# A down product by Strassen's identity in the last half of a two-layer decoder step

## The chip, the cores and the metric

The kernel runs on one core of one Trainium2 chip. The metric is the device time of one execution in microseconds (us), the median of several runs. TensorE is called PE in the profile, VectorE DVE, ScalarE ACT, GpSimd POOL and SyncE SP.

## The reference

One inference step of a hybrid decoder: 1024 prompt tokens and 8 sample tokens (1032 in all, `D_MODEL` 1024) go through a layer of convolution mixers and a layer of attention mixers, all in float32. Each is followed by an MLP with squared ReLU and `D_FF` = 4096:

```
def sqrelu_mlp(h, w1, w2):
    return jnp.square(jax.nn.relu(h @ w1)) @ w2
...
hp = hp + rmsnorm(sqrelu_mlp(rmsnorm(hp, g[2]), mlp_w1[layer], mlp_w2[layer]), g[3])
```

The change concerns the last of these MLPs, for the second half of the tokens, which ends the program.

## The kernel before

Features lie on partitions, tokens in the free dimension. The tokens are cut into three blocks, 512, 256 and 264 wide (`BW`). Half 0 is block 0, half 1 blocks 1 and 2. `Net.mlp` does one layer's MLP for one half and is called four times; the last call (half 1 of layer 1) is the last work of the program, save for the norm, the residual and the store.

Float32 matmuls are done in three: every operand is split into a high part of type fp32r (a cast on ACT) and a low part (what is left, a `tensor_sub` on DVE), and high by high, high by low and low by high are accumulated in one PSUM bank (`project`, and the same three lines in `down`). There are 41 buffers of 128 x 1056 (`unit`), 10 of 128 x 528 (`small`) and 8 PSUM banks.

`mlp` goes over the 4096 hidden features in eight chunks of 512, that is four tiles of 128. In a chunk `up` makes the four hidden tiles for the blocks of the half: 24 matmuls for each tile and block, then relu, square and the high part on ACT, the low part on DVE. Then `down` multiplies them with the chunk's four tiles of w2: eight output tiles `ct` for each block, 12 matmuls each. DVE adds each result from its bank to the accumulator `acc` in SBUF. The weights come by DMA in tiles of 128 x 1024 (`Weights`), are loaded up to three ahead and split up to two ahead. In the last chunk block 1 is finished first, up and down, and then block 2.

Every engine works through its instructions in the order in which they were emitted, and waits at the first whose operands aren't there. That order is set by `Pace`: an estimate of each engine's clock, from costs per element in `cost`. The main strand emits the matmuls; all else (splits, copies out of banks) are tasks, each of which goes on when the estimated clock of TensorE has passed the time that the task asked for. So where an instruction stands in its engine's queue is settled when the program is built. All of the kernel's instructions bear line 75, where `Engine` passes them on (line 77 in the changed kernel), and are told apart by the names of their tiles.

Of the kernel before, what the change touches and what calls it, by code (L numbers as in the profile page):

```python
# [10 lines left out]
F32 = mybir.dt.float32  # L11
# [6 lines left out]
P = 128  # L18
# [24 lines left out]
PE_NS, HOPS = 1.02 / 2400, 0.15  # L43

# [20 lines left out]
class Engine:  # L65
    """Passes calls on to an engine and keeps the estimate of its clock."""
# [20 lines left out]
class Pace:  # L87
    """Order of emission. Every engine issues its instructions in the order in which they are emitted, so
    independent strands of work are kept as tasks (generators), and a task goes on when the estimated clock
    of the tensor engine has reached the time that it asked for. The main strand is plain code."""  # L90
# [13 lines left out]
    def cost(engine, what, kw, aps):  # L104
# [14 lines left out]
        return 0.1 + n * 3.4 / 1000  # L119
# [44 lines left out]
    def soon(self):  # L164
        """when what was emitted last is ready"""
        return self.last + self.HOP
# [28 lines left out]
class Room:  # L195
    """Tiles of one size, given out and taken back by hand: the one that has been still for longest is next."""
# [17 lines left out]
class Feat:  # L214
    """Features of a block of tokens: units of KP feature tiles."""
# [9 lines left out]
class Weights:  # L225
    """The weights' tiles in the order of their use: loaded ahead, and split into high and low parts."""
# [7 lines left out]
    def advance(self):  # L234
        net, items = self.net, self.items
        while (self.loaded < len(items) and self.loaded - self.taken < self.limit
               and net.has_unit(self.back, 1 + 2 * self.whole)):
            src, n = items[self.loaded]
            x = net.take("raw", F32, self.back)
# [5 lines left out]
    def split(self, i, x, n):  # L245
# [9 lines left out]
        self.ready[i] = (h, l)  # L255

# [22 lines left out]

class Squares:  # L280
    """Sum of the squares of a block's feature tiles, by partition, as the tiles come."""
# [4 lines left out]
    def add(self, x, gain=None):  # L286
        """x: emitted last; scaled by the gain afterwards, where given"""
# [19 lines left out]
class Net:  # L307
# [29 lines left out]
    def weight_order(self):  # L337
# [7 lines left out]
        for i in range(2):  # L345
            for hf in range(2):
                for ch in range(NF // 4):
                    main.extend((io["w1"][i, 4 * ch + f], 1024) for f in range(4))
                    main.extend((io["w2"][i, 4 * ch + f], 1024) for f in range(4))
# [19 lines left out]
    def unit(self, name, dt=F32):  # L369
        """for the main strand"""  # L370
# [3 lines left out]
    def unit_later(self, name, dt=F32, back=True):  # L374
        """for tasks"""
# [39 lines left out]
    def bank_later(self, name="mm", spare=SPARE):  # L415
        """for tasks"""
# [4 lines left out]
    def table(self, name):  # L421
        """the set of the scalar engine's functions that follow"""
# [1455 lines left out]
```

## Time and profile before

| | us |
|---|---|
| three runs | 2210.55, 2209.44, 2217.82 (median 2210.55) |
| span of the profiled execution (no other time of it is given) | 2208.2 |
| TensorE busy | 2162.6 (98%) |
| DVE, ACT, POOL busy | 1481.2 (67%), 1084.4 (49%), 148.0 (7%) |
| TensorE's granted clock, mean of the span | 0.995 |

Busy time is a mean over stages. In the last half, which begins at 1824.9 us, the matmuls follow each other without a gap to 2195.1; then the last norm, residual and store. A matmul's own duration (0.28 us) is longer than its spacing, since they are pipelined; its price is the spacing.

### The profile page before, as it was taken

Reading aid. Unit: us, or ns where it says so; the run is one execution under the profiler, and the core shown is the slowest. Engines: PE = TensorE matmul, PEld = TensorE weight load, DVE = VectorE, ACT = ScalarE, POOL = GpSimd, SP = SyncE. Lnnn points to the kernel's source line nnn. Section 1 sums busy time; section 2 is a strip of 40 time slices with the busy share of each in tenths; the row PEclk is TensorE's granted clock in tenths of the full one; section 3 lists DMA queues with packets and bytes.
Section 4 is the critical chain, followed back from the end, with each engine's and each line's share of the span. In section 5 each row is a group of like instructions: output and inputs, shape, how many; then the busy total and the mean of one; then the engine's idle time right before and its main releaser. Section 6 shows DMA issues by size and latency. Waiting matters only on the chain. (4 is left out here: it accounts for less than half of the span.)

```text
span 2208.2 us, 35620 instructions
## 1 busy us (share of the span) xinstructions
PE 2162.6 (98%) x14039; PEld 1963.4 (89%) x14039; DVE 1481.2 (67%) x2762; ACT 1084.4 (49%) x2206; POOL 148.0 (7%) x253
## 2 busy tenths in 40 slices
PE   5999999999999999999999999999999999999997
PEld 4987898889888988999989989988887989999997
DVE  8885588984754756787658675667876585444446
ACT  6124354345543633788544463366874554334234
POOL 2131010010000011000000002201000000000000
PEclk9999999999999999999999999999999999999999
DMA  4113544352533444323343443532342455222231
GB/s 179 49 58 97 170 172 154 96 182 87 175 103 124 142 140 153 106 86 126 118 139 133 131 139 119 187 123 84 122 124 98 130 163 169 90 87 87 87 101 64
DMA packets 85255, 269.97 MB, mean 122 GB/s; under 512 B 16904, under 2 KB 19096, under 8 KB 84904
## 3 DMA queue, kind: packets, MB, share of 16 engines
q1 hardware_dynamic: 74528, 223.16, 31.5%
q0 software_dynamic: 10560, 44.54, 5.3%
q8 instruction: 110, 1.80, 0.3%
q14 instruction: 57, 0.47, 0.1%
HBM read 234.87 MB, written 44.83 MB: 127 GB/s over the span
## 5 line engine op out<-in xcount | busy, mean ns | idle before, releaser
L75 PE MATMUL mm<-xh,w 128*128 128x256 f32 (+2 forms) x4720 | 1086.8, 320 | 2.7 <-DVE xl L75 2.7
L75 PEld LDWEIGHTS mm<-xh,w 128*128 128x128 f32 x4720 | 788.6, 189 | 68.5 <-issue 2.9
L75 PE MATMUL mm<-hid,w 128*128 128x512 f32 (+2 forms) x4608 | 751.6, 321 | 0.0
L75 PE MATMUL mm<-xl,w 128*128 128x256 f32 (+2 forms) x2360 | 751.1, 318 | 0.0
L75 PEld LDWEIGHTS mm<-hid,w 128*128 128x128 f32 x4608 | 658.7, 188 | 65.5 <-issue 2.7
L75 DVE TENSOR_TENSOR w<-raw,w 128x1024 fp32r<-128x1024 f32 (+1 forms) x330 | 395.1, 1207 | 166.6 <-ACT w L75 166.4
L75 PEld LDWEIGHTS mm<-xl,w 128*128 128x128 f32 x2360 | 446.8, 189 | 31.5 <-issue 1.2
L75 ACT CAST w<-raw 128x1024 fp32r<-128x1024 f32 (+1 forms) x350 | 355.0, 1033 | 66.5 <-PE mm L75 44.5
L75 ACT ACTIVATE relu<-mm 128x256 f32<-128x256 f32 (+2 forms) x192 | 87.8, 457 | 408.6 <-PE mm L75 403.3
L75 DVE TENSOR_TENSOR acc<-acc,mm 128x256 f32<-128x256 f32 (+2 forms) x336 | 166.5, 508 | 133.8 <-PE mm L75 132.1
L75 DVE TENSOR_TENSOR hid<-mm,hid 128x256 fp32r<-128x256 f32 (+2 forms) x192 | 98.7, 514 | 219.8 <-ACT hid L75 219.0
L75 ACT ACTIVATE mm<-relu 128x256 f32<-128x256 f32 (+2 forms) x192 | 88.7, 462 | 6.1
L75 ACT ACTIVATE hid<-relu 128x256 fp32r<-128x256 f32 (+2 forms) x192 | 91.2, 475 | 0.0
L75 DVE SCALAR_TENSOR_TENSOR cv<-ga,small,cv 128x512 f32<-128x512 f32 x120 | 83.3, 744 | 0.0
L75 DVE SCALAR_TENSOR_TENSOR taps<-ga,small,taps 128x482 f32<-128x482 f32 (+29 forms) x120 | 78.6, 731 | 0.0
L75 ACT COPY qk<-mm 128x512 f32<-128x512 f32 (+2 forms) x39 | 17.4, 446 | 106.2 <-PE mm L75 101.3
L75 ACT COPY y<-mm 128x512 f32<-128x512 f32 (+2 forms) x48 | 21.4, 446 | 91.7 <-PE mm L75 91.7
L75 PE MATMUL mm<-mixh,w 128*128 128x512 f32 (+2 forms) x288 | 64.9, 320 | 0.0
L75 DVE TENSOR_TENSOR sq<-sq 128x264 f32<-128x264 f32 (+2 forms) x84 | 43.0, 512 | 29.9 <-ACT sq L75 29.0
L75 ACT CAST ph<-pt 128x512 fp32r<-128x512 f32 (+1 forms) x80 | 41.1, 522 | 34.8 <-PE pt L75 32.3
L75 ACT CAST xh<-norm 128x256 fp32r<-128x256 f32 (+2 forms) x104 | 41.4, 425 | 33.6 <-DVE norm L75 33.1
L75 POOL TENSOR_TENSOR w<-raw,w 128x1024 fp32r<-128x1024 f32 x20 | 50.5, 2543 | 108.3 <-ACT w L75 106.7
(235 smaller groups left out, 2091.6 us busy)
## 6 DMA issues: line engine op xcount, KB each, us to landing
raw<-w SPq DMA_DIRECT2D x256, 512.0 KB, 3.8
raw<-wic SPq DMA_DIRECT2D x32, 512.0 KB, 4.5
raw<-wia SPq DMA_DIRECT2D x26, 512.0 KB, 3.5
res<-res SPq DMA_DIRECT2D x18, 512.0 KB, 4.1
raw<-woc SPq DMA_DIRECT2D x16, 512.0 KB, 3.7
o_d_s<-c_d POOLq DMA_DIRECT2D x8, 1023.5 KB, 16.6
qscr<-qk POOLq DMA_DIRECT2D x26, 256.0 KB, 2.3
res<-y POOLq DMA_DIRECT2D x12, 512.0 KB, 3.9
```

What stands on the lines that cost most here:

```text
L75: r = fn(*args, **kw)
```

## The change

`FAST` says which chunks of which MLP half are done in the new way: of layer 1, half 1, chunks 0 to 6. In such a chunk the down product is taken as a product of 2 x 2 blocks, for each half `hc` of the output features: weights by two halves of the output columns and two halves of the chunk's hidden features (a11, a12, a21, a22), hidden tiles by two halves of the features and the two token blocks (r11, r12, r21, r22; block 1 is padded with zeros to 264). Strassen's identity in Winograd's form makes it with seven block products of sums instead of eight. `PRODUCTS` names them by the hidden side: 11, t1, 21, 22, t3, t2, t4.

`Weights.combine` loads two tiles of w2 for each `hc`, makes four sums on POOL, and splits the seven weight blocks (tiles `wp`): high part on ACT, low part on POOL and DVE in turn. `sums_chunk` leaves the squared hidden tiles in `hid`, makes four sums on DVE and splits the seven hidden blocks (tiles `t`). Each block product is 24 matmuls of 264 columns into two banks, and `collect` adds each bank to one of seven tiles `total` (in chunk 0 ACT copies it). After chunk 6 `join_totals` makes the accumulators from the totals with 14 sums on POOL. Chunk 7 is done as before. `Pace` counts a POOL operation at 2.5 ns an element in place of 3.4. Docstrings and comments went to blank lines, and `mlp` has the layer as a new argument; neither is shown.

```diff
+FAST = {(1, 1): (0, 7)}
+PRODUCTS = ("11", "t1", "21", "22", "t3", "t2", "t4")
...
-        return 0.1 + n * 3.4 / 1000
+        return 0.1 + n * 2.5 / 1000
...
+            if isinstance(src, tuple):
+                if not net.has_unit(self.back, 6 + 2 * self.whole):
+                    return
+                xs = [net.take("raw", F32, self.back) for _ in src]
+                for x, a in zip(xs, src):
+                    net.sp.dma_start(out=x[:, :n], in_=a)
+                self.whole += 2
+                self.ready[self.loaded] = parts = Parts(net)
+                net.pace.spawn(self.combine(self.loaded, xs, parts))
+                self.loaded += 1
+                continue
...
+    def combine(self, i, xs, parts):
...
+        net = self.net
+        yield net.pace.ready(*xs) + 0.1
+        while i - self.taken >= 4:
+            yield net.pace.now() + 0.3
+        block = lambda x, m: x[:, :1024].rearrange("p (f c) -> p f c", f=2)[:, :, m * 256:(m + 1) * 256]
+        a11, a21, a12, a22 = block(xs[0], 0), block(xs[0], 1), block(xs[1], 0), block(xs[1], 1)
+
+        def split(u, src):
+            h, l = parts.views(u)
+            net.act.copy(h, src)
+            yield net.pace.soon()
+            (net.dve if len(parts.units) % 2 else net.pool).tensor_sub(l, src, raw(h))
+            parts.units.append(u)
+
+        yield from split((yield from parts.unit()), a11)
+        small = yield from net.small("s1")
+        s1 = small[:, :512].rearrange("p (f c) -> p f c", f=2)
+        net.pool.tensor_add(s1, a21, a22)
+        net.pool.tensor_sub(a21, a11, a21)
+        at = net.pace.soon()
+        net.pool.tensor_sub(a11, s1, a11)
+        yield at
+        yield from split((yield from parts.unit()), s1)
+        net.drop(small)
+        u = yield from parts.unit()
+        yield from split(u, a12)
+        u = yield from parts.unit()
+        net.pool.tensor_sub(a12, a12, a11)
+        yield net.pace.soon()
+        yield from split(u, a12)
+        for src in (a21, a11, a22):
+            u = yield from parts.unit()
+            yield from split(u, src)
+        net.free(*xs)
+        self.whole -= 2
...
+class Parts:
...
+    DEPTH = 6
+
+    def __init__(self, net):
+        self.net, self.units, self.used, self.asked = net, [], 0, 0
+
+    def unit(self):
+        while self.asked - self.used >= self.DEPTH:
+            yield self.net.pace.now() + 0.2
+        self.asked += 1
+        return (yield from self.net.unit_later("wp", F32R, False))
+
+    @staticmethod
+    def views(u):
+        return [u[:, a * 512:(a + 1) * 512].rearrange("p (f c) -> p f c", f=2) for a in range(2)]
+
+    def get(self, n):
+        self.net.pace.wait(lambda: len(self.units) > n)
+        return self.views(self.units[n])
+
+    def done(self):
+        self.net.free(self.units[self.used])
+        self.used += 1
...
-                    main.extend((io["w2"][i, 4 * ch + f], 1024) for f in range(4))
+                    w2 = [io["w2"][i, 4 * ch + f] for f in range(4)]
+                    if self.fast(i, hf, ch):
+                        main.extend(((w2[hc], w2[hc + 1]), 1024) for hc in (0, 2))
+                    else:
+                        main.extend((w, 1024) for w in w2)
...
+    def mlp(self, layer, hf, xn, post, last=False):
         pace, W, bs = self.pace, self.W, HALVES[hf]
+        side_w = BW[bs[-1]] if hf else HT // 2
+        totals, outs = [], []
...
+        def sums_chunk(ch, first):
...
+            n = side_w
+            us, hi, lo, ready, raws, squared = {}, {}, {}, set(), {}, [0]
+            view = lambda u, o=0: u[:, o:o + 2 * n].rearrange("p (f t) -> p f t", f=2)
+
+            def raw_block(k):
+                s = yield from self.small("hid")
+                raws[k] = s
...
+            def hidden(f, b, ps):
+                yield pace.soon()
+                a = ps
+                self.act.activation(a, ps, AF.Relu)
+                yield pace.soon()
+                if hf:
+                    yield from squares(f, b - 1, a)
...
+            def split(k, src):
+                u = us[k] = yield from self.unit_later("t", F32R, False)
+                hi[k], lo[k] = view(u), view(u, 2 * n)
+                yield from self.split_later(hi[k], lo[k], src)
+                ready.add(k)
+
+            def left():
+                while squared[0] < 4:
+                    yield pace.now() + 0.2
+                yield pace.soon()
+                small = yield from self.small("t1")
+                t1 = view(small)
+                self.dve.tensor_sub(t1, view(raws["12"]), view(raws["11"]))
+                yield from split("11", view(raws["11"]))
+                yield from split("t1", t1)
+                self.drop(small)
+
+            def right():
+                while squared[0] < 8 or "11" not in ready:
+                    yield pace.now() + 0.2
+                yield pace.soon()
+                r11, r12, r21, r22 = (view(raws[k]) for k in ("11", "12", "21", "22"))
+                yield from split("21", r21)
+                self.dve.tensor_sub(r12, r22, r12)
+                yield from split("22", r22)
+                self.drop(raws["22"])
+                self.dve.tensor_add(r11, r12, r11)
+                self.dve.tensor_sub(r21, r21, r11)
+                yield pace.soon()
+                for k, t in (("t3", "12"), ("t2", "11"), ("t4", "21")):
+                    yield from split(k, view(raws[t]))
+                    self.drop(raws[t])
...
+            def collect(total, ps):
+                def emit():
+                    if first:
+                        self.act.copy(total, ps)
+                    else:
+                        self.dve.tensor_add(total, total, ps)
+                    self.banks.give(ps)
+
+                outs.append(pace.then(emit))
...
+            if first:
+                totals.extend(self.unit("total") for _ in PRODUCTS)
+            for hc in range(2):
+                parts = W.get()
+                for m, k in enumerate(PRODUCTS):
+                    h, l = parts.get(m)
+                    pace.wait(lambda: k in ready)
+                    bank = None
+                    for q in range(2):
...
+                            bank = self.bank()
...
+                        for f in range(2):
+                            wh, wl = (v[:, f, q * P:(q + 1) * P] for v in (h, l))
+                            self.pe.matmul(ps, lhsT=wh, rhs=hi[k][:, f], start=f == 0, stop=False)
+                            self.pe.matmul(ps, lhsT=wh, rhs=lo[k][:, f], start=False, stop=False)
+                            self.pe.matmul(ps, lhsT=wl, rhs=hi[k][:, f], start=False, stop=f == 1)
+                            pace.tick()
+                        if hf:
+                            collect(totals[m][:, (2 * hc + q) * n:(2 * hc + q + 1) * n], ps)
+                    if not hf:
...
+                    parts.done()
+                    if hc:
+                        self.free(us[k])
...
+        def join_totals(first):
...
+            pace.wait(lambda: all(t.done for t in outs))
+            if first:
+                for b in bs:
+                    acc[b] = self.feat(b, KD, "acc")
+            add, sub = self.pool.tensor_add, self.pool.tensor_sub
+            for hc in range(2):
+                m1, m5, m2, m3, m7, m6, m4 = (t[:, hc * 2 * n:(hc + 1) * 2 * n].rearrange("p (q t) -> p q t", q=2)
+                                              for t in totals)
...
+                def to(rows, side, x, y):
+                    if hf:
+                        v = acc[bs[side]].v[hc][:, 2 * rows:2 * rows + 2]
...
+                    c = slice(0, v.shape[-1])
+                    if first:
+                        add(v, x[:, :, c], y[:, :, c])
...
+                to(0, 0, m2, m1)
+                add(m6, m6, m1)
+                add(m5, m5, m6)
+                to(0, 1, m3, m5)
+                to(1, 1, m5, m7)
+                add(m7, m7, m6)
+                to(1, 0, m4, m7)
+            self.free(*totals)
...
+            if self.fast(layer, hf, ch):
+                at_start = ch == FAST[layer, hf][0]
+                sums_chunk(ch, at_start)
+                if not self.fast(layer, hf, ch + 1):
+                    join_totals(FAST[layer, hf][0] == 0)
+                continue
```

What it does to the order of instructions, at three places.

DVE before, in a middle chunk of the last half, from the low part of the last hidden tile (`hid`) to the first adds of the down product. `w` are low parts of weights, `acc` the adds from PSUM banks `mm`:

```order
L75 TENSOR_TENSOR hid_20351<-mm_20386,hid_20351 128x264
L75 TENSOR_TENSOR w_20428<-raw_20416,w_20427 128x1024
L75 TENSOR_TENSOR w_20431<-raw_20349,w_20430 128x1024
L75 TENSOR_TENSOR acc_18862<-acc_18862,mm_20420 128x256
L75 TENSOR_TENSOR acc_18864<-acc_18864,mm_20421 128x264
L75 TENSOR_TENSOR acc_18862<-acc_18862,mm_20422 128x256
```

DVE in the change, a middle chunk, from the first add after the up product. `mm_19998` and `mm_20009` are the two tiles of product 11, `mm_20021` and `mm_20030` those of t1; `t_20043` is hidden block 21:

```order
L77 TENSOR_TENSOR total_18863<-total_18863,mm_19998 128x264
L77 TENSOR_TENSOR total_18864<-total_18864,mm_20021 128x264
L77 TENSOR_TENSOR w_20004<-raw_19937,w_20003 128x1024
L77 TENSOR_TENSOR total_18863<-total_18863,mm_20009 128x264
L77 TENSOR_TENSOR total_18864<-total_18864,mm_20030 128x264
L77 TENSOR_TENSOR wp_20018<-raw_19855,wp_20018 128x512
L77 TENSOR_TENSOR t_20043<-hid_19921,t_20043 128x528
```

Before, the low part of the last hidden tile came ahead of all adds of the down product; now the low part of hidden block 21 comes behind four of them, a low part of w1 and one of block weights.

DVE in the change, right behind that. `t_20051` is block 22, `t_20091` t3, `hid` the sums, `mm_20053` and `mm_20066` product 21, `mm_20075` product 22:

```order
L77 TENSOR_TENSOR hid_19798<-hid_19990,hid_19798 128x528
L77 TENSOR_TENSOR t_20051<-hid_19990,t_20051 128x528
L77 TENSOR_TENSOR hid_19755<-hid_19798,hid_19755 128x528
L77 TENSOR_TENSOR hid_19921<-hid_19921,hid_19755 128x528
L77 TENSOR_TENSOR wp_20058<-raw_19854,wp_20058 128x512
L77 TENSOR_TENSOR total_18865<-total_18865,mm_20053 128x264
L77 TENSOR_TENSOR total_18865<-total_18865,mm_20066 128x264
L77 TENSOR_TENSOR total_18866<-total_18866,mm_20075 128x264
L77 TENSOR_TENSOR t_20091<-hid_19798,t_20091 128x528
```

All of it is new: three sums, three adds and a weights' low part stand between the low parts of 22 and of t3.

POOL in the change, the end of the same chunk's work (before, POOL has no such work in the last half). `wp_19909` and `wp_20025` are the fifth and the seventh weight block of the first `hc`, `wp_19996`, `wp_20047` and `wp_20177` the third, fifth and seventh of the second:

```order
L77 TENSOR_TENSOR wp_19909<-raw_19776,wp_19909 128x512
L77 MEMSET hid_19921 128x2x8
L77 TENSOR_TENSOR wp_19996<-raw_19855,wp_19996 128x512
L77 TENSOR_TENSOR raw_19855<-raw_19855,raw_19854 128x2x256
L77 TENSOR_TENSOR wp_20025<-raw_19777,wp_20025 128x512
L77 TENSOR_TENSOR wp_20047<-raw_19854,wp_20047 128x512
L77 TENSOR_TENSOR wp_20177<-raw_19855,wp_20177 128x512
```

Of the chunk's 16 operations, 13 stand before the low part of `wp_20025`, whose cast comes behind the end of the up product, as do those of the last two.

## Rows read from the trace of the kernel before

**Rows 1.** Head of the page: span, busy time and instructions of each engine.
```profile
span 2208.2 us, 35620 instructions
PE 2162.6 (98%) x14039; PEld 1963.4 (89%) x14039; DVE 1481.2 (67%) x2762; ACT 1084.4 (49%) x2206; POOL 148.0 (7%) x253
```
**Rows 2.** Windows, last half: length, busy PE, PEld, DVE, ACT, POOL, clock, DMA, GB/s.
```profile
1871.00:2148.00 277.00, 277.00 (x2307) 277.00 (x2307) 115.48 (x191) 100.39 (x194) 0.00 (x0) 1.00 0.27 92
```
**Rows 3.** Chain that ended last: start, length, what.
```profile
1831.31 343.01 PE mm L75 x2856
```
**Rows 4.** Timeline of PE, one chunk: start, duration, instruction.
```profile
1917.78 0.28 PE L75 MATMUL mm<-xh,w 128*128 128x256 f32 x1
...
1920.75 0.28 PE L75 MATMUL mm<-xl,w 128*128 128x264 f32 x1
...
1923.31 0.28 PE L75 MATMUL mm<-xl,w 128*128 128x264 f32 x1
...
1963.89 0.29 PE L75 MATMUL mm<-xh,w 128*128 128x256 f32 x1
```
**Rows 5.** Timeline of DVE: operations back to back, five sizes.
```profile
1752.19 1.28 DVE L75 TENSOR_TENSOR y<-y,res 128x512 f32<-128x512 f32 x2
...
1945.70 1.50 DVE L75 TENSOR_TENSOR acc<-acc,mm 128x256 f32<-128x256 f32 x4 [0.19 <-PE mm L75]
...
1952.92 2.35 DVE L75 TENSOR_TENSOR w<-raw,w 128x1024 fp32r<-128x1024 f32 x2
...
2199.64 0.71 DVE L75 TENSOR_TENSOR acc<-acc,rstd 128x528 f32<-128x528 f32 x1
2200.38 0.71 DVE L75 TENSOR_TENSOR acc<-acc,res 128x528 f32<-128x528 f32 x1
2201.01 0.70 DVE L75 TENSOR_TENSOR acc<-acc,rstd 128x528 f32<-128x528 f32 x1
```
**Rows 6.** Timeline of POOL, first stage: pairs of operations.
```profile
18.21 5.24 POOL L75 TENSOR_TENSOR w<-raw,w 128x1024 fp32r<-128x1024 f32 x2 [13.50 <-ACT w L75]
...
102.47 4.76 POOL L75 TENSOR_TENSOR w<-raw,w 128x1024 fp32r<-128x1024 f32 x2 [17.84 <-ACT w L75]
...
177.79 5.57 POOL L75 TENSOR_TENSOR w<-raw,w 128x1024 fp32r<-128x1024 f32 x2
```
**Rows 7.** Groups by form, ACT: count, busy us, mean ns, idle before.
```profile
L75 ACT ACTIVATE mm<-relu 128x264 f32<-128x264 f32 x32 | 12.7, 396 | 1.0
L75 ACT ACTIVATE relu<-mm 128x264 f32<-128x264 f32 x32 | 12.5, 391 | 54.9 <-PE mm L75 54.9
...
L75 ACT CAST mixh<-f 128x512 fp32r<-128x512 f32 x12 | 7.1, 590 | 13.6 <-DVE f L75 13.5
```
**Rows 8.** Timeline of DVE beside the pairs of rows 6.
```profile
19.02 2.25 DVE L75 SCALAR_TENSOR_TENSOR norm<-x,small,rstd 128x256 f32<-128x256 f32 x1
21.18 2.83 DVE L75 TENSOR_TENSOR total<-total,sq 128x512 f32<-128x512 f32 x1
...
104.05 0.43 DVE L75 TENSOR_TENSOR ga<-mm,ga 128x264 f32<-128x264 f32 x1
...
178.86 5.05 DVE L75 TENSOR_TENSOR total<-total,sq 128x512 f32<-128x512 f32 x2
```
**Rows 9.** Timeline of PE, two idle times (in brackets) and their releasers.
```profile
42.23 0.39 PE L75 MATMUL mm<-xh,w 128*128 128x256 f32 x1 [2.67 <-DVE xl L75]
...
183.97 1.22 PE L75 MATMUL st<-total,ones 128*128 128x512 f32 x1 [2.36 <-DVE total L75]
```
**Rows 10.** Windows behind these idle times, columns as in rows 2.
```profile
43.60:50.40 6.80, 5.40 (x24) 4.91 (x23) 6.70 (x18) 6.34 (x11) 0.00 (x0) 0.50 0.09 37
183.60:187.00 3.40, 3.03 (x5) 1.81 (x6) 0.91 (x2) 0.89 (x2) 0.00 (x0) 0.50 0.00 0
```
**Rows 11.** Timeline of DVE, a weights' low part in the last chunk.
```profile
2159.30 1.23 DVE L75 TENSOR_TENSOR w<-raw,w 128x1024 fp32r<-128x1024 f32 x1 [0.52 <-ACT w L75]
```

More of the change, by code (lines that the diff above doesn't have):

```diff
@@ L356, in weight_order, with fast @@
         return main, back
+    @staticmethod
+    def fast(layer, hf, ch):
+        first, last = FAST.get((layer, hf), (0, 0))
+        return first <= ch < last
     def has_unit(self, back, n=1):
@@ L636, in copy_out @@
             sums.add(y)
-    def mlp(self, hf, xn, post, last=False):
+    def mlp(self, layer, hf, xn, post, last=False):
         pace, W, bs = self.pace, self.W, HALVES[hf]
+        side_w = BW[bs[-1]] if hf else HT // 2
+        totals, outs = [], []
         at = {b: slice(OFF[b] - OFF[bs[0]], OFF[b] - OFF[bs[0]] + BW[b]) for b in bs}
@@ L686, in down, with squares @@
                             sums[b].add(a, self.gain(7, ct) if final and b == NB - 1 else None)
+        def sums_chunk(ch, first):
[5 more added lines that the diff above has]
+                raws[k] = s
+                if hf and k in ("11", "21"):
+                    self.pool.memset(view(s)[:, :, BW[1]:n], 0.0)
+            def squares(f, side, a):
+                k = f"{f // 2 + 1}{side + 1}"
+                if k not in raws:
+                    yield from raw_block(k)
+                self.act.square(view(raws[k])[:, f % 2, :a.shape[-1]], a)
+                squared[0] += 1
+            def hidden(f, b, ps):
[6 more added lines that the diff above has]
+                else:
+                    for side in range(2):
+                        yield from squares(f, side, a[:, side * n:(side + 1) * n])
+                self.banks.give(ps)
[29 more added lines that the diff above has]
+                    self.drop(raws[t])
+            pace.spawn(left())
+            pace.spawn(right())
+            for f in range(4):
+                w = W.get()
+                for b in bs:
+                    ps = self.projected(BW[b], w, xn[b][0])
+                    pace.spawn(hidden(f, b, ps))
+                W.done(w)
+            def collect(total, ps):
+                def emit():
+                    if first:
+                        self.act.copy(total, ps)
+                    else:
+                        self.dve.tensor_add(total, total, ps)
+                    self.banks.give(ps)
+                outs.append(pace.then(emit))
[8 more added lines that the diff above has]
+                    for q in range(2):
+                        if hf or q == 0:
+                            bank = self.bank()
+                        ps = bank[:, :n] if hf or q == 0 else bank[:, n:2 * n]
+                        for f in range(2):
[7 more added lines that the diff above has]
+                    if not hf:
+                        collect(totals[m][:, hc * 2 * n:(hc + 1) * 2 * n], bank)
+                    parts.done()
+                    if hc:
+                        self.free(us[k])
@@ new lines, in join_totals @@
+        def join_totals(first):
+            n = side_w
+            pace.wait(lambda: all(t.done for t in outs))
+            if first:
+                for b in bs:
+                    acc[b] = self.feat(b, KD, "acc")
[6 more added lines that the diff above has]
+                        v = acc[bs[side]].v[hc][:, 2 * rows:2 * rows + 2]
+                    else:
+                        v = acc[0].v[2 * hc + rows][:, :, side * n:(side + 1) * n]
+                    c = slice(0, v.shape[-1])
+                    if first:
+                        add(v, x[:, :, c], y[:, :, c])
+                    else:
+                        add(x[:, :, c], x[:, :, c], y[:, :, c])
+                        add(v, v, x[:, :, c])
+                to(0, 0, m2, m1)
[6 more added lines that the diff above has]
+            self.free(*totals)
@@ L1758, in build @@
         for hf in range(2):
-            net.mlp(hf, xn[0], after[0])
+            net.mlp(0, hf, xn[0], after[0])
             net.pace.spawn(net.attn(hf, xn[1], join))
         for hf in range(2):
-            end = net.mlp(hf, xn[2], after[1], hf == 1)
+            end = net.mlp(1, hf, xn[2], after[1], hf == 1)
         net.pace.wait(lambda: end.done)
```

## The prediction

> **What bounds the kernel now.** I read the page first, then the last stretch in windows, then the chain of waits, then timelines of single engines. The page has TensorE busy for 98% of 2208.2 us [rows 1]. In the steady part of the last MLP half the window row shows TensorE busy for all of its 277 us at full clock, with 2307 matmuls, DVE busy 42%, ACT 36% and POOL not at all [rows 2]. The chain that ended last is one piece of matmuls there, 343.0 us long, with no other engine in it [rows 3]. So TensorE sets the end, a matmul taken away is worth its spacing, and the other engines have room on average. Whether they have it at the right moment is the question of this change.
>
> **What it removes.** One chunk takes 46.11 us from first matmul to first matmul (1917.78 to 1963.89), for 192 matmuls of 256 and 192 of 264 columns [rows 4]. The 264-column ones stand 2.56 us / 21 = 0.1219 us apart [rows 4]; what is left makes the others 0.1183. The down product of a chunk is 96 of each: 23.06 us. Seven products in place of eight are 168 matmuls, all 264 wide (block 1 is padded): 20.48 us. That is 2.58 us a chunk and 18.0 us for seven.
>
> **What it adds on DVE and POOL.** Per chunk DVE adds up 28 products from PSUM in place of 16, makes four sums and seven low parts of hidden blocks, four low parts of w1 and six of the block weights. Its spacings: 0.36 us for a 264-wide add from PSUM (1.50 for four, the last one 0.42), 1.13 for a 1024-wide low part, 0.60 for 512, 0.63 for 528, 0.74 where it needs the result just before it [rows 5]. 28 x 0.36 + 4 x 1.13 + 6 x 0.60 + 11 x 0.63 = 25.1 us of some 44: no bound by itself. POOL does 16 sums or low parts of 512 per chunk. Two of 1024 took 4.76 us, so one of 512 some 1.19, and a chunk 19 us [rows 6]. That fits too.
>
> **The wait it adds.** Let T be the end of a chunk's up product. The order of DVE after T is: add of product 11's first tile, add of t1's first tile, low part of the next w1 tile, the two second tiles, a low part of block weights, and only then the low part of hidden block 21, which the third product needs. DVE issues in that order, so the add of t1's first tile, which can't begin before T + 18 x 0.1219 + 0.16 = 2.35 us (0.16 by which a matmul outlasts its spacing), holds all behind it, though ACT has the high part of 21 ready at about T+2.9 (relu 0.39, square 0.40, three casts of 0.59 [rows 7], and 0.2 of hop). From T+2.35: 0.36 + 1.13 + 0.36 + 0.36 + 0.60 + 0.70 (result included) = T+5.86. TensorE wants it for its 26th matmul, T + 25 x 0.1219 = T+3.05. It waits 2.81 us, and every later product stands behind it.
>
> The second wait: after 21's low part DVE issues the sum for t3, the low part of 22, two more sums (the second needs the first), a weights' low part, three adds from PSUM, and then t3's low part. Starts: 5.79, 6.42, 7.05, 7.79, 8.42, then 9.02 to 10.10, and t3's low part is there at T+10.80. TensorE does the rest of 21 and 22 (23 x 0.1219 = 2.80 us) by T+8.66 and wants it at T+8.78: 2.02 us. The parts for t2 and t4 follow at 0.63 and are in time. In the second four columns of tiles everything but the block weights is there, and DVE's backlog of adds is gone before eight banks are full, so I cost it at nothing. Both waits: 4.83 us a chunk, more than the 2.58 saved. Bounds: nothing if the adds and low parts came in time as the averages have it, 7 us if ACT too is late (its weight casts stand in front of 21's high part).
>
> **POOL beside DVE.** At 19.02 a DVE operation that reads two tiles in SBUF took 2.25 us, and at 21.18 an add 2.83, both under two POOL operations that ran from 18.21 to 23.45 (5.24 for two in place of 4.76); at 178.86 two adds took 5.05 under the POOL pair from 177.79 [rows 6, 8]. Alone such an add takes some 0.7 [rows 5]. So each waits for the whole operation of the other. By the Trainium skill, page "SBUF — State Buffer", section "Who interferes with whom", a DVE instruction with two SBUF inputs and a GpSimd one that reads SBUF exclude each other for a whole instruction; the trace agrees in the rows just named, and without that rule the next term would be nothing and the sum 2231. Adds from PSUM have one SBUF input; one of these at 104.05 kept its 0.43, and the POOL pair around it its 4.76 [rows 6, 8]. Between T and T+6 POOL has the low parts of two weight blocks to make. The first falls while DVE waits for t1's tile. The second, ready at about T+3.2, is held by the 1024-wide low part until T+3.84, ends at 5.03 and holds the next one, due at 4.56: 0.47 us more. Bounds 0, and 4.8 if POOL is so late that four of its operations of 1.19 fall there.
>
> **The clock.** TensorE idle for 2.67 us before 42.23, and for 2.36 before 183.97 (there behind the very DVE add that POOL held up) [rows 9], was each time followed by a granted clock of 0.50, 1.2 in place of 2.4 GHz, for 6.8 and 3.4 us [rows 10]. The new first wait is as long as these. A half-speed stretch of 3.4 us costs 1.7, but if it falls on products 21 and 22 it only fills the second wait of 2.02. I take 0.5 a chunk, near that case; the bounds are 0 and 3.4.
>
> **First chunk, join and tail.** In chunk 0 ACT copies the products out, and its copies and casts stand before 21's high part in the same way; I take the same wait (0 to 7). The POOL sums that join the totals, 14 x 1.2 = 17 us, run under chunk 7: block 1's columns 2-3, 4-5 and 6-7 are ready after 7, 8 and 14 of them, TensorE comes to the last ones after 11.4 us of up product and some 10 of down. Hidden. But chunk 7's low parts of weights now meet POOL. Before, one of them began at 2159.30 and ended at 2160.53 [rows 11], and TensorE, whose down product began at 1963.89 + 4 x 46.11 + 11.36 = 2159.7, wanted it at about 2160.6: one POOL operation ahead of it costs about 1 us (0 to 4.8 for four). The instructions of all engines before the last half keep their order but for a few places, and the DMA loads stay eight of 512 KB a chunk, so I cost these at nothing.
>
> **Sum.** 7 x (-2.58 + 4.83 + 0.47 + 0.50) = 22.5, and 1.0 for the tail: 23.5 us. The profiled execution's span is 2208.2; the page gives no time of its own around it, and the median of the three runs, 2210.55, is 2.35 above it. 2208.2 + 23.5 + 2.35 = 2234 us.
>
> **Rivals.**
> 1. The waits don't come: DVE and ACT run ahead, as their averages of 42% and 36% would let them [rows 2], and the whole of TensorE's saving shows: 2210.6 - 18.0 + 1 = 2193. Against it: the queue's order, in which 21's low part stands behind an add that waits for t1. It holds while both waits together stay well under 2.58 a chunk.
> 2. Half of the waits: 2.4 a chunk (the second one filled, or the first one shorter), which cancels the saving: 2210.6 + 7 x (2.4 + 0.47 - 2.58) + 1 = 2214.
> 3. The clock decides: each chunk's wait is followed by the longer half-speed stretch, 3.4 us lost a chunk in place of 0.5: 2234 + 7 x 2.9 = 2254. For it: both rows [rows 10]. Against it: matmuls at half speed give DVE time to catch up. The Trainium skill, page "TensorE: Matmul & The Clock Gate", section "HAM oscillation — how this bites in real kernels", tells of a kernel that fell to half clock again in every turn of its loop; the two rows agree with a single fall each, and by that rule this rival is the likelier one.
> 4. The lock decides: POOL falls behind in the up product (16 operations against 21 of DVE that read two tiles) and four of its operations stand between T and T+6: 7 x 4.3 = 30 more, 2264. It decides once POOL's queue is not empty at T. For it: rows 6 and 8; against: POOL's 13 operations before T are 15.5 us of the 23 there.
>
> **Chances.** Forecast with its bounds (2222 to 2246) 0.50, rival 3 with what lies near it 0.14, rival 4 0.06, rival 2 0.17, rival 1 0.13. Within 0.5% of 2210.55, about what a measurement of this kernel can tell from no change, is 2199.5 to 2221.6: faster 0.13, same 0.17, slower 0.70. The range, 2204 to 2256, leaves out most of rival 1 and the far end of 4; the forecast's own is 2222 to 2246.
>
> **What would show it.** In the changed profile each of the chunks 1 to 6 should last some 49 us from first to first up matmul, with TensorE waiting about 3 us for the DVE tile t before the third product and about 2 before the fifth; DVE adds of total and low parts back to back between; granted clock under 1.00 in those stretches; DVE rows of 528 and 512 with means above 0.70. If TensorE is at 100% there and chunks last 43.5 us, my reading of the queue is wrong; if waits stand elsewhere (weights wp, total at the join), the place is.

## The result, and the profile after

The changed kernel took 2248.84 us (median of five runs, 2248.32 to 2255.74) against 2212.38 for the kernel before (median of five, 2209.44 to 2217.82): ratio 1.0173, 95% interval 1.0157 to 1.0189. It is slower, as forecast, by 36.5 us where 23.5 were forecast. The time lies above the forecast's own bounds (2222 to 2246) and inside the range of 2204 to 2256; the nearest of the times on record is rival 3's 2254.

The page's head, to be read beside [rows 1]: TensorE's busy time rose by 8.9 us though it has 168 matmuls fewer, a first sign of a lower clock; DVE's rose by 128.3 and POOL's by 197.9.

```profile
span 2254.0 us, 35683 instructions
PE 2171.5 (96%) x13871; PEld 1965.1 (87%) x13871; DVE 1609.5 (71%) x2869; ACT 1118.0 (50%) x2281; POOL 345.9 (15%) x393
```

Two profiled executions can differ ahead of the change. That of the changed kernel is the longest of its five, 2255.74 us. Its last half begins 6.1 us later (first up matmul at 1831.06 against 1824.93), and the window row of 1400 to 1500 us shows where most of this arises: the same busy share, but a clock of 0.93 instead of 1.00. The first row is of the kernel before, the second of the changed one (columns as in [rows 2]).

```profile
1400.00:1500.00 100.00, 99.43 (x640) 88.69 (x639) 65.95 (x159) 49.06 (x121) 15.92 (x48) 1.00 0.43 142
```
```profile
1400.00:1500.00 100.00, 99.43 (x606) 87.60 (x606) 60.23 (x147) 47.33 (x114) 10.33 (x29) 0.93 0.42 140
```

In the ten profiles of this document the half begins between 1823.6 and 1832.3 us, though TensorE, DVE and ACT have the same order of work ahead of it in all of them: this is scatter, not the change. So the sharp measure is the length of the last half, from its first up matmul to the end of the span: 383.3 us before, 422.9 after, 39.7 more. Cut at the first up matmul of chunk 0, chunk 1 and chunk 7, the windows of the changed kernel are:

```profile
1831.06:1894.03 62.97, 49.54 (x363) 47.67 (x362) 45.76 (x39) 31.04 (x71) 28.42 (x22) 0.89 0.32 110
1894.03:2193.90 299.87, 277.86 (x2162) 273.92 (x2161) 221.46 (x293) 125.44 (x248) 160.63 (x115) 0.95 0.26 83
2193.90:2254.00 60.10, 47.64 (x390) 46.81 (x388) 38.99 (x72) 26.34 (x58) 12.07 (x9) 0.93 0.23 82
```

Chunk 0 lasts 62.97 us (before 46.64): 16.3 more. Chunks 1 to 6 last 49.98 each (before 46.14): 3.84 more each, 23.0 in all. Chunk 7 with the end lasts 60.10 (before 59.77): 0.3 more. The one piece of 343 us in the chain [rows 3] is now broken once a chunk:

```profile
1928.84 39.95 PE mm L77 x329
1973.42 45.59 PE mm L77 x353
```

TensorE's timeline shows the idle time in brackets. The first two rows are the first and second product of chunk 0, the last three are chunk 3, whose up product ends at T = 2016.64:

```profile
1863.98 3.01 PE L77 MATMUL mm<-t,wp 128*128 128x264 f32 x12 [9.18 <-DVE t L77]
1869.41 2.07 PE L77 MATMUL mm<-t,wp 128*128 128x264 f32 x11 [2.43 <-DVE t L77]
...
2020.23 0.39 PE L77 MATMUL mm<-t,wp 128*128 128x264 f32 x1 [0.52 <-ACT t L77]
2023.67 4.71 PE L77 MATMUL mm<-t,wp 128*128 128x264 f32 x24 [3.05 <-DVE t L77]
2028.67 5.50 PE L77 MATMUL mm<-t,wp 128*128 128x264 f32 x41 [0.29 <-DVE t L77]
```

In chunk 3 TensorE is idle for 3.57 us in all at the third product, where the forecast put it. From start to start, the product's second matmul comes at T + 7.03, 3.98 us behind its turn at T + 3.05. Before the fifth only 0.29 us is left, but the 24 matmuls between (of products 21 and 22, twelve each for the first `hc`) took 4.71 us where 24 took 3.19 at full clock (run 3 below), since the granted clock of that stretch was 0.66 (columns as in [rows 2]):

```profile
2023.60:2028.67 5.07, 4.71 (x24) 4.50 (x24) 4.96 (x11) 3.69 (x6) 0.24 (x1) 0.66 0.01 5
```

DVE's timeline in the same place is the order that the prediction read, beside POOL's. The low part of w takes 1.95 us (1.23 in [rows 11]) over POOL's operation from 2018.96, and the low part wp 1.08 over the one from 2020.78:

```profile
2019.38 1.95 DVE L77 TENSOR_TENSOR w<-raw,w 128x1024 fp32r<-128x1024 f32 x1
2021.25 0.76 DVE L77 TENSOR_TENSOR total<-total,mm 128x264 f32<-128x264 f32 x2
2021.92 1.08 DVE L77 TENSOR_TENSOR wp<-raw,wp 128x512 fp32r<-128x512 f32 x1
2022.92 0.70 DVE L77 TENSOR_TENSOR t<-hid,t 128x528 fp32r<-128x528 f32 x1
```
```profile
2017.71 1.29 POOL L77 TENSOR_TENSOR raw<-raw 128x512 f32<-128x512 f32 x1
2018.96 1.28 POOL L77 TENSOR_TENSOR wp<-raw,wp 128x512 fp32r<-128x512 f32 x1
2020.78 1.67 POOL L77 TENSOR_TENSOR wp<-raw,wp 128x512 fp32r<-128x512 f32 x1 [0.54 <-ACT wp L77]
```

Chunk 0 has something more: under its up product DVE still does the post-norm of half 0 (newton, acc), in operations that read two tiles in SBUF, and POOL now makes the first block weights at the same time. DVE and then POOL, in the changed kernel:

```profile
1838.85 1.67 DVE L77 SCALAR_TENSOR_TENSOR newton<-newton,rstd 128x512 f32<-128x512 f32 x1
...
1842.25 3.37 DVE L77 SCALAR_TENSOR_TENSOR acc<-acc,small,rstd 128x512 f32<-128x512 f32 x2
...
1847.79 2.30 DVE L77 TENSOR_TENSOR acc<-acc,res 128x1024 f32<-128x1024 f32 x1
...
1858.87 1.22 DVE L77 TENSOR_TENSOR acc<-acc,res 128x1024 f32<-128x1024 f32 x1
...
1863.22 0.70 DVE L77 TENSOR_TENSOR t<-hid,t 128x528 fp32r<-128x528 f32 x1
```
```profile
1838.68 1.29 POOL L77 TENSOR_TENSOR wp<-raw,wp 128x512 fp32r<-128x512 f32 x1 [20.03 <-ACT wp L77]
...
1846.74 2.27 POOL L77 TENSOR_TENSOR s<-raw 128x512 f32<-128x512 f32 x1
1849.09 2.16 POOL L77 TENSOR_TENSOR raw<-raw 128x512 f32<-128x512 f32 x1
```

While POOL works, the same operation on acc and res takes 2.30 us, after it 1.22; the low part that the very first product needs comes only at 1863.22, and TensorE has waited 9.18 us for it.

### The profile page after: what moved, and what is told of

The parts are those of the page before. It is cut to its first block, busy times and chain, and to the rows that moved or that the text cites. A ratio compares the mean times of both kernels' runs of the same rounds, so it can differ in the third digit from the quotient of the medians.

```text
span 2254.0 us, 35683 instructions
## 1 busy us (share of the span) xinstructions
PE 2171.5 (96%) x13871; PEld 1965.1 (87%) x13871; DVE 1609.5 (71%) x2869; ACT 1118.0 (50%) x2281; POOL 345.9 (15%) x393
## 5 line engine op out<-in xcount | busy, mean ns | idle before, releaser
L77 PE MATMUL mm<-hid,w 128*128 128x512 f32 (+2 forms) x3264 | 589.8, 337 | 0.0
L77 PEld LDWEIGHTS mm<-hid,w 128*128 128x128 f32 x3264 | 497.5, 189 | 65.6 <-issue 2.7
L77 PE MATMUL mm<-t,wp 128*128 128x264 f32 x1176 | 167.3, 306 | 35.4 <-DVE t L77 31.4
L77 PEld LDWEIGHTS mm<-t,wp 128*128 128x128 f32 x1176 | 160.9, 208 | 41.2 <-DVE t L77 35.4
L77 DVE TENSOR_TENSOR acc<-acc,mm 128x512 f32<-128x512 f32 (+2 forms) x240 | 127.9, 545 | 72.8 <-PE mm L77 70.8
L77 DVE TENSOR_TENSOR hid<-mm,hid 128x512 fp32r<-128x512 f32 (+2 forms) x136 | 74.9, 551 | 129.4 <-ACT hid L77 128.6
L77 POOL TENSOR_TENSOR wp<-raw,wp 128x512 fp32r<-128x512 f32 x56 | 88.3, 1578 | 174.3 <-ACT wp L77 174.3
L77 DVE TENSOR_TENSOR total<-total,mm 128x264 f32<-128x264 f32 x168 | 67.1, 424 | 35.0 <-PE mm L77 34.7
L77 ACT ACTIVATE mm<-relu 128x512 f32<-128x512 f32 (+2 forms) x136 | 66.8, 491 | 4.3
L77 ACT ACTIVATE hid<-relu 128x512 fp32r<-128x512 f32 (+2 forms) x136 | 68.6, 504 | 0.0
## 6 DMA issues: line engine op xcount, KB each, us to landing
o_d_s<-c_d POOLq DMA_DIRECT2D x8, 1023.5 KB, 16.8
```

The lines of the kernel that those rows point to most:

```text
L77: r = fn(*args, **kw)
```

## The experiments

Eight kernels ran. Their halves, cut as above (us; after: 2248.8, the kernel before of each batch: 2213.6 for the first four, 2210.1 for the others, which ran on another chip):

| kernel | median | ratio to before (95%) | half | chunk 0 | chunks 1-6, each | chunk 7 and end |
|---|---|---|---|---|---|---|
| before | 2212.4 | | 383.3 | 46.6 | 46.1 | 59.8 |
| after | 2248.8 | 1.0173 (1.0157-1.0189) | 422.9 | 63.0 | 50.0 | 60.1 |
| 1 chunk 0 old | 2229.7 | 1.0073 (1.0059-1.0087) | 400.3 | 46.6 | 48.6 | 62.4 |
| 2 parts first | 2255.9 | 1.0194 (1.0180-1.0209) | 426.8 | 61.8 | 50.9 | 59.6 |
| 3 no POOL reads | 2227.8 | 1.0073 (1.0061-1.0085) | 399.6 | 49.7 | 48.4 | 59.6 |
| 4 chunk 0 old, parts first | 2245.0 | 1.0147 (1.0134-1.0160) | 416.9 | 46.6 | 51.3 | 62.8 |
| 5 no POOL reads, parts first | 2202.9 | 0.9966 (0.9955-0.9978) | 373.8 | 47.4 | 44.4 | 60.1 |
| 6 sums on DVE | 2233.3 | 1.0102 (1.0087-1.0116) | 401.5 | 55.5 | 47.7 | 59.6 |
| 7 sums on DVE, parts first | 2207.7 | 0.9985 (0.9976-0.9994) | 379.6 | 55.3 | 44.1 | 59.6 |
| 8 as 7, chunk 0 old | 2197.7 | 0.9944 (0.9932-0.9957) | 370.3 | 46.6 | 43.5 | 62.6 |

An edit can move more than it names, since `Pace` settles the order of every queue anew. Run 3 alone has the changed kernel's order on TensorE, DVE and ACT from the first instruction to the last; in the others DVE's order differs from chunk 0 on.

**1. Chunk 0 in the old way.**

```
-FAST = {(1, 1): (0, 7)}
+FAST = {(1, 1): (1, 7)}
```

> The seven products are used in chunks 1 to 6 only; chunk 0 is the old one, and the join adds to its result. Theory (the loss of the first chunk, 63.0 us against 46.1 in the two profiles, comes from the post-norm of half 0 that runs on DVE under it and meets POOL's sums): chunk 0 falls back to 46 us, the chunk that is now first among the seven products costs the 49.9 us of the others, and the time is 2248.8 - 17 = some 2232 us (2226 to 2238; a join that adds to what is there has 28 POOL sums in place of 14, and a late one would cost a few us). Rival (the loss belongs to whichever chunk is the first with seven products, because ACT copies its products out and stands late with the casts): chunk 1 takes some 60 us in place of chunk 0, and the time is 2244 to 2250 us.

2229.7 us. Chunk 0 is back at 46.6, and chunk 1, now the first with seven products, took 48.8: the rival is out, the loss belongs to the place, not to being first. The join, which now adds to what is there with 22 sums (not 28) in place of 14, costs chunk 7 some 2.6 us.

The time is as forecast, but not by chunk 0 alone. The half is 22.6 us shorter than after: 16.4 in chunk 0, 8.5 in chunks 1 to 6, and 2.3 given back in chunk 7. The 8.5 were not forecast. The order moved: in chunk 3, whose up product ends at T = 2000.22, DVE has after T neither a low part of w nor one of wp ahead of the low part of hidden block 21 (here the add before it, and it):

```profile
2003.34 0.43 DVE L77 TENSOR_TENSOR total<-total,mm 128x264 f32<-128x264 f32 x1 [0.30 <-PE mm L77]
2003.69 0.70 DVE L77 TENSOR_TENSOR t<-hid,t 128x528 fp32r<-128x528 f32 x1
```

It starts at T + 3.47 there, at T + 6.28 in the changed kernel, and TensorE's waits are 1.02, 0.59 and 2.14 us. So with POOL's reads in place a chunk in another order took 1.4 us less, still too long: chunks 3 to 6 take 48.2, against 46.1 before.

**2. The parts of 21 and 22 ahead of the adds.**

```
+                if f == 3 and k == "21":
+                    squared.append(k)
...
-                while squared[0] < 8 or "11" not in ready:
+                while "21" not in squared or "11" not in ready:
...
-                yield from split("21", r21)
+                yield from split("21", view(raws["21"]))
+                while squared[0] < 8:
...
+                    if hc == 0 and m == 0:
+                        pace.wait(lambda: "22" in ready)
```

> Only the order of issue is changed: the parts of hidden block 21 are made as soon as its own two squares are there, and DVE issues the low parts of 21 and 22 before the adds of products 11 and t1. Theory (the wait of 3.5 us before the third product is the queue's order, and the half clock behind it is its consequence): both go, chunks 1 to 6 take 43.5 to 45 us in place of 49.9, the granted clock stays at 1.00 there, chunk 0 keeps its loss, and the time is 2248.8 - 6 x 5.4 = some 2216 us (2212 to 2226). Rival (DVE has no room in the first 10 us of a down product, whatever the order): the wait only moves to t3, t2 or t4 or to the banks that wait for the adds, chunks 1 to 6 take 48 to 50 us, and the time is 2240 to 2250 us.

The theory failed: 2255.9 us, 50.9 a chunk. The rival named what came, a wait for the banks, but the time is above its bounds too. The long wait before the third product became one of 0.6, and another came right behind it, for a bank that an add (total) should have emptied (TensorE, then DVE, in one chunk):

```profile
2013.36 2.84 PE L77 MATMUL mm<-t,wp 128*128 128x264 f32 x18 [0.59 <-DVE t L77]
...
2019.64 0.56 PE L77 MATMUL mm<-t,wp 128*128 128x264 f32 x1 [2.84 <-DVE total L77]
```
```profile
2009.28 2.32 DVE L77 TENSOR_TENSOR w<-raw,w 128x1024 fp32r<-128x1024 f32 x1
2011.52 1.79 DVE L77 TENSOR_TENSOR t<-hid,t 128x528 fp32r<-128x528 f32 x1
...
2015.07 3.48 DVE L77 TENSOR_TENSOR hid<-hid 128x528 f32<-128x528 f32 x2
```

Two sums of hidden blocks took 3.48 us where [rows 5] let one expect 0.63 + 0.74 = 1.4. With the operations that long, DVE has no room for this order.

**3. POOL reads nothing.** In `combine` every sum and low part of POOL becomes a `memset` of the same tile, so the kernel leaves these sums out and part of TensorE's operands are zeros.

```
-        net.pool.tensor_add(s1, a21, a22)
-        net.pool.tensor_sub(a21, a11, a21)
+        net.pool.memset(s1, 0.0)
+        net.pool.memset(a21, 0.0)
```

> POOL's sums and low parts of the block weights are left out: in their place POOL writes zeros to the same tiles, so that it reads nothing; DVE keeps its own low parts. Theory (DVE operations that read two SBUF tiles and POOL's exclude each other): the DVE operations of chunk 0 that take 1.67 to 2.3 us fall to 0.65 to 1.2, its waits of 9.2 and 2.4 us go, which with the clock is 13 to 17 us; chunks 1 to 6 keep the wait for the low part of 21 at about the forecast 2.8 us and lose 0.5 to 1 us each; the time is some 2230 us (2224 to 2236). Rival (the DVE queue of chunk 0 is long by itself): chunk 0 stays over 58 us, DVE's durations fall but the wait does not, and the time is 2240 to 2249 us.

2227.8 us, as the theory had it: 21.0 less by the medians. The half is 23.3 us shorter than after, 13.3 of them in chunk 0 and 1.6 in each of chunks 1 to 6 (the theory had 0.5 to 1). Groups of DVE by form from 1894 to 2150 us (count, busy us, mean ns), first of the changed kernel, then of this one:

```profile
L77 DVE TENSOR_TENSOR total<-total,mm 128x264 f32<-128x264 f32 x140 | 56.3, 425 | 30.5 <-PE mm L77 30.2
L77 DVE TENSOR_TENSOR w<-raw,w 128x1024 fp32r<-128x1024 f32 x21 | 33.8, 1609 | 35.7 <-ACT w L77 35.7
L77 DVE TENSOR_TENSOR t<-hid,t 128x528 fp32r<-128x528 f32 x30 | 31.1, 1064 | 0.0
L77 DVE TENSOR_TENSOR wp<-raw,wp 128x512 fp32r<-128x512 f32 x20 | 26.2, 1329 | 0.0
```
```profile
L77 DVE TENSOR_TENSOR total<-total,mm 128x264 f32<-128x264 f32 x145 | 59.2, 427 | 57.3 <-PE mm L77 57.3
L77 DVE TENSOR_TENSOR w<-raw,w 128x1024 fp32r<-128x1024 f32 x21 | 25.6, 1220 | 27.7 <-ACT w L77 27.7
L77 DVE TENSOR_TENSOR t<-hid,t 128x528 fp32r<-128x528 f32 x32 | 21.6, 701 | 0.0
L77 DVE TENSOR_TENSOR wp<-raw,wp 128x512 fp32r<-128x512 f32 x22 | 15.1, 686 | 2.7 <-ACT wp L77 2.7
```

Each of these operations with two inputs in SBUF loses its surplus; the add from PSUM, with one, never had any (425 and 427 ns). The changed kernel alone shows the same in its chunks 1 to 6: the 20 low parts of t that overlap a sum or low part of POOL take 1.41 us on average, the 16 that overlap none 0.70; of the adds from PSUM, 39 that overlap take 0.42, and 128 that don't 0.43. In run 3 seven sums of hidden blocks lie beside a `memset` and take 0.70 us, as they do alone. That is also how the Trainium skill puts it, page "SBUF — State Buffer", section "Who interferes with whom": a DVE instruction with two SBUF inputs contends with a GpSimd one that reads SBUF, not with one that only writes; the rows agree.

This run also shows what the clock does. TensorE in two chunks, with the granted clock behind the first wait below (0.65 in the first chunk, 1.00 in the second):

```profile
1953.43 4.63 PE L77 MATMUL mm<-t,wp 128*128 128x264 f32 x24 [2.70 <-DVE t L77]
1958.35 3.92 PE L77 MATMUL mm<-t,wp 128*128 128x264 f32 x30 [0.28 <-DVE t L77]
...
2001.87 3.19 PE L77 MATMUL mm<-t,wp 128*128 128x264 f32 x24 [2.71 <-DVE t L77]
2006.70 9.50 PE L77 MATMUL mm<-t,wp 128*128 128x264 f32 x76 [1.64 <-DVE t L77]
```
```profile
1953.40:1958.10 4.70, 4.63 (x24) 4.42 (x24) 4.67 (x9) 3.36 (x6) 0.57 (x2) 0.65 0.12 48
...
2001.80:2005.10 3.30, 3.19 (x24) 2.98 (x24) 3.27 (x7) 1.94 (x4) 0.58 (x2) 1.00 0.28 114
```

The same wait was followed by a fall in one and by none in the other. Where the clock fell, the 24 matmuls took 1.44 us longer and the second wait was 1.36 shorter; the two chunks last 48.4 and 48.3 us. Half clock there only fills the second wait. Of chunks 1 to 6, three fell (48.4 to 48.6 us) and three did not (48.3 each); why the one and not the other stays open.

**4. Edits 1 and 2 together.**

```
-FAST = {(1, 1): (0, 7)}
+FAST = {(1, 1): (1, 7)}
...
+                        pace.wait(lambda: "22" in ready)
```

> Both edits together: chunk 0 old, and the low parts of 21 and 22 ahead of the adds. Theory (two separate losses, one in chunk 0 and one in each later chunk): the gains add up, 2248.8 - 17 - 32 = some 2200 us, below the kernel before (2196 to 2208). Rival (one of the two losses is taken over by something else, the lock with POOL's sums or the banks): 2215 to 2232 us, no faster than the kernel before.

The theory failed: 2245.0 us, 51.3 a chunk, 2.7 more than with edit 1 alone. The rival was right that the gains don't add up, but the time is 13 us above its bounds. With POOL's reads in place edit 2 gains nothing.

**5. No POOL reads, parts first.** As 3, with the early part of 21 as in 2, and t3 made right behind 22:

```
                 yield from split("22", r22)
                 self.drop(raws["22"])
+                yield from split("t3", r12)
                 self.dve.tensor_add(r11, r12, r11)
```

> POOL's sums and low parts are left out as in the run without POOL reads, and the order of issue is changed: low parts of 21 as soon as its squares are there, then 22 and t3, ahead of the adds of the first products. Theory (two causes in a row: POOL holds every DVE operation that reads two SBUF tiles, and DVE's order puts adds ahead of the parts; with the lock gone DVE has room, so the order decides alone): the waits of 2.70 and 1.65 us go, chunks 1 to 6 take 43.5 to 44.5 us in place of 48.4, granted clock 1.00, and the time is 2227.8 - 6 x 4.3 - 2 = some 2200 us (2195 to 2208), the saving of seven products seen for the first time. Rival (the first 10 us of a down product have more DVE work than fits, lock or not): the wait moves to t2, t4 or to banks that wait for adds, chunks 1 to 6 take 47 us or more, and the time is 2220 us or more.

2202.9 us and 44.4 a chunk, clock 1.00, as the theory had it. The order alone (2) gave +0.9 a chunk, the lock alone (3) -1.6, both together with the step for t3 -5.6: more than the two apart. (The step for t3 is in 5, 7 and 8 alone, so what it adds by itself stays open.)

**6. The same sums on DVE, old order.**

```
-            (net.dve if len(parts.units) % 2 else net.pool).tensor_sub(l, src, raw(h))
+            net.dve.tensor_sub(l, src, raw(h))
...
-        net.pool.tensor_add(s1, a21, a22)
+        net.dve.tensor_add(s1, a21, a22)
```

> All of the computation, with the sums and low parts of the block weights on DVE in place of POOL, and the order of the hidden parts as in the change. Theory (POOL's help costs more than its work: 16 operations of 0.62 us are 10 us more for DVE, which POOL's reads take from it anyway): chunk 0 falls from 63 to some 50 us, chunks 1 to 6 to 48 to 49 us with the same first wait of 2.7 us, time some 2229 us (2224 to 2234). Rival (DVE becomes the bound: 25.1 + 10 us of work in a chunk, in an order that keeps the hidden parts behind it): chunks 1 to 6 take 51 us or more, time 2245 us or more.

2233.3 us. Chunks 1 to 6 take 47.7, 2.2 less than after, though DVE has 16 operations a chunk more. (Chunks 1 to 5 take 47.3; chunk 6, where POOL already makes the first nine sums of the join, 49.9.) With nothing left out of the computation the low parts of t take 0.70 us and those of w 1.22 in chunk 3. But the first wait is 1.63 us, not 2.7: the low part of 21 starts at T + 4.1, at T + 5.2 in run 3, so a part of the gain is order and not the engine, and the two are not told apart here. Chunk 0 stays at 55.5, where the theory said 50: post-norm and sums now stand one behind the other on DVE.

**7. Sums on DVE, parts first**, 6 with the order of 5.

```
-        net.pool.tensor_sub(a12, a12, a11)
+        net.dve.tensor_sub(a12, a12, a11)
...
+                yield from split("t3", r12)
```

> All of the computation, sums and low parts of the block weights on DVE, and the parts of 21, 22 and t3 issued ahead of the adds. Theory: neither lock nor order is left, chunks 1 to 6 take 43.7 to 45 us, chunk 0 48 to 52, time some 2206 us (2198 to 2214), at or below the kernel before. Rival (35 us of DVE work in a chunk of 44 leave the parts late in the first 10 us after the up product): chunks 47 to 50 us, time 2225 us or more.

2207.7 us, 44.1 a chunk, as the theory had it; chunk 0, at 55.3 where the theory had 48 to 52, takes back most of it.

**8. As 7, chunk 0 old.**

```
-FAST = {(1, 1): (0, 7)}
+FAST = {(1, 1): (1, 7)}
```

> The same with chunk 0 the old one, so six chunks of seven products; the join adds to what is there, with 28 POOL sums under chunk 7. Theory: chunk 0 46.6 us, chunks 1 to 6 43.7 to 45, chunk 7 some 2.6 us longer as in the first run with chunk 0 old, time some 2203 us (2197 to 2210), below the kernel before. Rival (as in the kernel without the edit of the order, waits stay at 3 us or more a chunk): 2222 us or more.

2197.7 us, ratio 0.9944: faster than both. Its windows, cut as above:

```profile
1825.49:1872.05 46.56, 46.56 (x387) 46.47 (x386) 26.20 (x34) 23.41 (x50) 2.34 (x7) 1.00 0.49 168
1872.05:2133.22 261.17, 260.86 (x2162) 260.65 (x2161) 208.22 (x360) 136.50 (x276) 12.62 (x17) 1.00 0.28 94
2133.22:2195.80 62.58, 47.91 (x390) 46.72 (x388) 42.62 (x73) 25.67 (x58) 26.15 (x17) 0.91 0.24 85
```

TensorE is idle for 0.31 us in six chunks. One takes 261.17 / 6 = 43.53, which is 46.11 - 2.58, the arithmetic of the saving. 6 x 2.61 = 15.7 are won, 2.8 go back in chunk 7, where the join now makes 22 POOL sums instead of 14: 12.9 by the profile, 12.4 by the medians.

## Why the prediction was right and where it fell short

The direction and the steady chunks came by the mechanism that was forecast; of the signs named ahead, all came but the idle time before the fifth product, which the half clock filled in most chunks. That the time still lies in the range is owed in part to its width: the largest single loss, in chunk 0, is not in the sum.

**The saving of 2.58 a chunk** was right: the eighth run shows it whole.

**The two waits** were right in place and size. From start to start, in chunk 3 without POOL's reads, the third product came 2.87 us late (forecast 2.81; idle 2.70) and, at full clock, the fifth 1.90 later still (2.02; idle 1.64). With POOL's reads the first was 3.98, forecast 2.81 + 0.47 = 3.28. The second was filled by the half clock, as the prediction took it: from 2023.67 to 2028.67 are 5.00 us, 2.07 more than 24 matmuls need at full clock (24 x 0.122).

**The clock** was priced at 0.5 a chunk. In chunk 3 (49.83 us) 43.53 + 3.98 + 2.07 leave 0.25 for it and all else; by the same sum, with the mean of the six chunks (49.98), 0.40. Rival 3 was right that the falls come in every chunk (in the 4.5 us behind the first wait the granted clock was 0.50 to 0.62 in all six), but not that they would fall on time that was lost anyway. That its 2254 lies nearest to the measured time is chance: the surplus is chunk 0's.

**The lock in chunks 1 to 6** was too small: 50.0 - 48.4 = 1.6 instead of 0.47. The prediction counted two low parts between T and T+6, and had POOL done with 13 operations by T. In chunk 3 the thirteenth, a sum, ends only at T + 2.36 (2017.71 + 1.29). So the first of the two low parts, which was to fall into DVE's wait, holds the low part of w, and the second holds wp: the low part of 21 starts 1.12 us later than in run 3 (T + 6.28 and T + 5.16). That is most of the 1.6. POOL is late because the two slow each other in the up product: its thirteen operations follow each other from 1998.12 on and take 1.61 us each; at the 1.29 of one alone they would end at 2014.9, before T, by estimate. DVE's surplus is spread: it is busy for 221.5 us in the six chunks, for 161.4 without POOL's reads, so 10 us a chunk. The windows of the up product alone (chunk 3 of the changed kernel, then of run 3) show where most of it lies, hidden behind matmuls that need nothing from DVE, 15.44 us against 7.51:

```profile
1993.67:2016.64 22.97, 22.97 (x195) 22.97 (x193) 15.44 (x10) 12.44 (x27) 18.13 (x13) 1.00 0.06 23
```
```profile
1972.95:1995.95 23.00, 23.00 (x195) 23.00 (x193) 7.51 (x10) 12.44 (x27) 5.82 (x13) 1.00 0.06 22
```

Together a chunk lost 3.84 against 3.22 forecast, 3.7 us in six.

**Chunk 0** is the step that failed. "I take the same wait (0 to 7)" looked at ACT's copies alone; chunk 0 lost 16.3 us, of which 13.3 are the lock (run 3). That DVE still works through the post-norm of half 0 under this up product, in operations of the form that rows 8 had shown to be held, could be read from the DVE timeline of the kernel before, where the same work ran undisturbed:

```profile
1834.04 0.69 DVE L75 SCALAR_TENSOR_TENSOR newton<-newton,rstd 128x512 f32<-128x512 f32 x1
...
1839.43 1.41 DVE L75 SCALAR_TENSOR_TENSOR acc<-acc,small,rstd 128x512 f32<-128x512 f32 x2
...
1849.41 1.21 DVE L75 TENSOR_TENSOR acc<-acc,res 128x1024 f32<-128x1024 f32 x1
```

Rival 4 had the mechanism, the lock with a POOL whose queue isn't empty at T, but looked for it in the steady chunks, where that came and cost 1.6 us, not its 4.3. Chunk 0 is 13.1 us above its forecast of 3.2, and with the 3.7 above it makes 16.8; the tail, 0.3 instead of 1.0, takes 0.7 off. That is 16.1, and 23.5 + 16.1 = 39.6, the 39.7 by which the half grew in the profile. The medians differ by 36.5.

**The join** was hidden, as forecast, as long as it makes the accumulators (0.3 us): eight of its 14 sums already run in chunk 6. Where it adds to them, chunk 7 is 2.6 to 3.0 us longer (runs 1, 4 and 8).

## What to carry to other kernels

An engine that is busy for 40% can still decide the time in the ten microseconds behind a dependency: write down its queue there, instruction by instruction, and do this for the first turn of a loop as well, where the tail of the stage before still runs. Moving work from DVE to POOL was no relief here, where both read SBUF with two-input operations: moving 16 operations a chunk back to DVE made the kernel faster, in part through the order that came with it. When a fix of the order alone gains nothing, test it again with the second cause removed before dropping it; here no order brought a chunk under the 46.1 of before while POOL read, and no run without POOL's reads did in the old order. And compare the order that was built with the one that was meant: run 1 moved more than it named.

## What the runs showed of the hardware that was not expected

- DVE adds with one input in PSUM keep 425 ns beside POOL's sums, while a 1024-wide low part goes from 1.22 to 1.61 us on average and a 512-wide one from 0.69 to 1.33.
- POOL pays too: one of its operations of 512 columns takes 1.29 us, and up to 2.27 beside DVE's (the row at 1846.74).
- An equal wait of TensorE is not always followed by half clock: 2.70 us was followed by 0.65 in one chunk, 2.71 by 1.00 in the next of the same run. Two windows of 100 us with the same 0.57 us of idle time had 1.00 and 0.93.
